# A decoder layer on one Trainium2 core: in the seven-product pairs, two of the four weight sums formed by an adding transfer instead of VectorE, more such pairs, and another order of pairs in the last matrix

## The chip, the core and the metric

The kernel runs on one core of a Trainium2 chip. The metric is device time in microseconds (us) of one execution, as the median over several executions. The engines have short names here: PE is TensorE, DVE is VectorE, ACT is ScalarE, POOL is GpSimd, and SP is SyncE, which issues nearly all of the DMA transfers. Every engine works through its own instructions strictly in program order, and an instruction whose semaphores have not come holds up all that stand behind it on that engine.

## The reference

One layer, 256 tokens, width 2048, all in float32. What matters here are its matrix products:

```python
h = rms_norm(x, mix_norm)
proj = h @ w_in                                  # attention, LRU and SSM inputs, and four gates of 2048 columns
gates = sigmoid(gate_logits)                     # (256, 4, 2048)
merged = sum(gates[b] * (branches[b] @ w_branch[b]) for b in range(4))
x = x + merged @ w_out
hf = rms_norm(x, ffn_norm)
gate, up = split(hf @ w_ffn_in)                  # 5632 columns each
return x + (silu(gate) * up) @ w_ffn_out         # 5632 -> 2048
```

## The kernel before

All weights are streamed once from HBM, and PE multiplies them with activations that stay in on-chip memory. Every product of two float32 numbers is made of three matmuls in a reduced format: a weight tile `wr` is split by ACT into a rounded part `wh` (line 209) and by DVE into the rest `wl` = `wr` - `wh` (line 214). The activations are split likewise, and PE adds up high·high, high·low and low·high (lines 202 to 204). One matmul takes 128 rows of the sum and 512 output columns for 128 tokens.

Gates, `w_ffn_in` and `w_ffn_out` go through `stream_pairs`. One step of it is a *pair* p: 256 rows of the inner dimension by 1024 columns, 1 MB, seen as a 2x2 block of weights `raw[:,0..3]` (128 rows by 512 columns each), against a 2x2 block of activations (two row blocks, two token blocks of 128). A *plain* pair makes the 2x2 block product with eight block products, that is 24 matmuls. A *seven* pair (p in `seven`) makes it with seven block products, 21 matmuls, as in Strassen's and Winograd's schemes. For that it needs sums of activation blocks, formed once, and four sums of weight blocks, formed for each pair: the tile `ws` (`t13`, one DVE instruction over 1024 columns, line 227), and two more of 512 columns each that overwrite `raw[:,0]` (line 233) and `raw[:,1]` (line 234). The four split steps of a seven pair are named a, b, c, d; `wl_fo_17c` is the split of `ws` of pair 17 in `w_ffn_out`, `wl_fo_17d` that of the two sums in `raw`. The first products of a seven pair use a and b; the fourth and fifth use c; the last two use d. Seven pairs collect four of their products in banks `m1`, `m5`, `m6`, `m7`, which are added into the results after the last seven pair of the column half (`shared_products`, and `mid` with lines 1125 to 1133 for `w_ffn_out`).

Stages: gates in eight stages (`ps_g`), each followed by a branch product (`ps_b`); then `w_out`; `w_ffn_in` in eleven steps j with eight pairs each (`fi`); `w_ffn_out` in two column halves, c = 0 and c = 1, of 22 pairs each (`fo`). `PLAN_GATE`, `SEVEN_IN`, `SEVEN_OUT` and `PLAN_OUT` are hand-written tables of the order of pairs and of which are seven pairs. A scheduler interleaves the instructions on each engine after them; weight work has high priority. Weight tiles come through three buffers (`wraw`), the split tiles through four of each kind. Activation sums for `w_ffn_out` are stored to HBM as they are formed (`sums`, line 1047) and read back two pairs at a time into `sr` (line 1111), then split into `sx_hi` and `sx_lo` (lines 1112, 1113). The residual is loaded whole into `x2o` (line 1100), and after each column half DVE adds the four result banks to it (line 1140), which also makes those banks free for the next half; line 1142 stores them.

Of the kernel before, what the change touches and what calls it, by code (L numbers as in the profile page):

```python
# [1240 lines left out]
```

## Time and profile before

| what | us |
|---|---|
| three runs: median (lowest to highest) | 1876.64 (1875.7 to 1876.91) |
| the profiled execution, its whole time | 1875.47 |
| span of the profiled execution | 1873.5 |
| PE busy | 1855.8, 99% of the span |
| DVE busy | 1414.0, 75% |
| ACT busy | 963.6, 51% |
| POOL busy | 175.3, 9% |
| mean DMA rate | 196 GB/s |

The profiled execution is 1.2 us below the median, and 2.0 us of its time lie outside the span. Matmuls are pipelined, so PE's busy time says that a matmul was in flight, not that PE was at its peak rate. A wait is listed with the instruction that ended last before the waiting one could start.

### The profile page before, as it was taken

How to read it: one execution, taken by the hardware profiler on the slowest of the kernel's cores; microseconds unless marked ns; L12 is line 12 of the kernel's file. 1: busy time of each engine (PE TensorE's matmuls, PEld its weight loads, DVE VectorE, ACT ScalarE, POOL GpSimd, SP SyncE). 2: the span in 40 equal slices, each digit the busy share in tenths (PEclk: the TensorE clock that was granted, in tenths of full speed). 3: DMA queues.
4: the chain of work that ended last, by engine and by line, in shares of the span. 5: the costliest groups of instructions: out<-in, count | busy, mean ns of one | idle time of the engine just before them, and what ended most of it. 6: DMA issues, size and time to landing. Idle time of an engine off the chain costs nothing.

```text
span 1873.5 us, 22243 instructions
## 1 busy us (share of the span) xinstructions
PE 1855.8 (99%) x8546; PEld 1546.1 (83%) x8546; DVE 1414.0 (75%) x1730; ACT 963.6 (51%) x1200; POOL 175.3 (9%) x152
## 2 busy tenths in 40 slices
...
GB/s 298 205 158 165 167 205 166 167 187 180 176 178 162 175 202 201 181 180 225 202 245 182 202 185 239 182 182 213 200 193 217 214 200 193 208 251 221 181 223 135
DMA packets 64567, 367.56 MB, mean 196 GB/s; under 512 B 7952, under 2 KB 17484, under 8 KB 23244
## 3 DMA queue, kind: packets, MB, share of 16 engines
...
## 4 chain that ended last, share of the span: by engine, by line
PE 96%; DVE 2%; DMA 1%; issue 0%; ACT 0%; SPq 0%; DVEq 0%
PE ps_fi L202 7%; PE ps_fi L203 7%; PE ps_fi L204 7%; PE ps_att L169 6%; PE ps_att L167 6%; PE ps_att L168 6%; PE ps_g L202 5%; PE ps_g L204 5%; PE ps_g L203 5%; PE ps_fo L202 3%; PE ps_fo L204 3%; PE ps_fo L203 3%; PE ps_b L203 2%; PE ps_b L204 2%; PE ps_b L202 2%; PE ps_ssm L167 2%
## 5 line engine op out<-in xcount | busy, mean ns | idle before, releaser
L161 DVE TENSOR_TENSOR wl_att<-wr_att,wh_att 128x1024 fp32r<-128x1024 f32 x128 | 159.6, 1250 | 92.5 <-ACT wh_att L159 92.3
L159 ACT ACTIVATE wh_att<-wr_att 128x1024 fp32r<-128x1024 f32 x128 | 135.4, 1060 | 163.9 <-PE ps_att L169 145.2
L167 PE MATMUL ps_att<-wh_att,hT_hi 128*128 128x512 f32 x512 | 206.6, 403 | 0.0
L169 PE MATMUL ps_att<-wh_att,hT_lo 128*128 128x512 f32 x512 | 200.2, 391 | 0.0
L168 PE MATMUL ps_att<-wl_att,hT_hi 128*128 128x512 f32 x512 | 199.8, 390 | 0.0
L169 PEld LDWEIGHTS ps_att<-wh_att,hT_lo 128*128 128x128 f32 x512 | 96.1, 188 | 20.7
L168 PEld LDWEIGHTS ps_att<-wl_att,hT_hi 128*128 128x128 f32 x512 | 96.4, 188 | 19.0
L167 PEld LDWEIGHTS ps_att<-wh_att,hT_hi 128*128 128x128 f32 x512 | 96.3, 188 | 18.8
L980 POOL TENSOR_TENSOR mg<-mg,gt 128x512 f32<-128x512 f32 x24 | 39.2, 1663 | 435.2 <-DVE gt L978 435.2
L167 PE MATMUL ps_ssm<-wh_ssm,hT_hi 128*128 128x384 f32 (+2 forms) x160 | 57.1, 357 | 7.3 <-ACT hT_hi L306 7.3
L161 DVE TENSOR_TENSOR wl_o<-wr_o,wh_o 128x1024 fp32r<-128x1024 f32 x32 | 40.8, 1281 | 26.2 <-ACT wh_o L159 26.1
L159 ACT ACTIVATE wh_o<-wr_o 128x1024 fp32r<-128x1024 f32 x32 | 33.8, 1060 | 48.3 <-PE ps_o L169 39.9
L784 POOL TENSOR_TENSOR sq_t<-tk_t 128x512 f32<-128x512 f32 (+3 forms) x32 | 32.5, 1025 | 272.2 <-ACT tk_t L779 272.0
L168 PE MATMUL ps_ssm<-wl_ssm,hT_hi 128*128 128x384 f32 (+2 forms) x160 | 56.5, 353 | 0.0
L169 PE MATMUL ps_ssm<-wh_ssm,hT_lo 128*128 128x384 f32 (+2 forms) x160 | 56.4, 353 | 0.0
L167 PE MATMUL ps_o<-wh_o,mT_hi 128*128 128x512 f32 x128 | 50.9, 397 | 0.0
L169 PE MATMUL ps_o<-wh_o,mT_lo 128*128 128x512 f32 x128 | 50.0, 391 | 0.0
L168 PE MATMUL ps_o<-wl_o,mT_hi 128*128 128x512 f32 x128 | 49.9, 390 | 0.0
L159 ACT ACTIVATE wh_ssm<-wr_ssm 128x768 fp32r<-128x768 f32 (+2 forms) x40 | 35.2, 889 | 26.0 <-PE ps_ssm L169 17.5
L161 DVE TENSOR_TENSOR wl_ssm<-wr_ssm,wh_ssm 128x768 fp32r<-128x768 f32 (+2 forms) x40 | 40.2, 1014 | 8.9 <-ACT wh_ssm L159 8.7
L159 ACT ACTIVATE wh_lru<-wr_lru 128x1024 fp32r<-128x1024 f32 x24 | 25.4, 1059 | 29.2 <-PE ps_lru L169 21.1
L167 PE MATMUL ps_lru<-wh_lru,hT_hi 128*128 128x512 f32 x96 | 39.3, 409 | 0.0
...
## 6 DMA issues: line engine op xcount, KB each, us to landing
wr_fi<-in_w_ffn_in SPq DMA_DIRECT2D x88, 1024.0 KB, 4.8
wr_att<-in_w_in SPq DMA_DIRECT2D x64, 1024.0 KB, 4.7
wr_g<-in_w_in SPq DMA_DIRECT2D x64, 1024.0 KB, 4.7
wr_fo<-in_w_ffn_out SPq DMA_DIRECT2D x44, 1024.0 KB, 5.0
wr_b<-in_w_branch SPq DMA_DIRECT2D x24, 1024.0 KB, 4.8
wr_o<-in_w_out SPq DMA_DIRECT2D x16, 1024.0 KB, 4.7
wr_lru<-in_w_in SPq DMA_DIRECT2D x12, 1024.0 KB, 4.7
...
```

The costliest lines, as they stand in the source:

```text
L159: A.activation(wh, rk, AF.Copy)
L161: V.tensor_tensor(wl, rk, wh.bitcast(F32), op=ALU.subtract)
L167: PE.matmul(o_ps, xh, wh[:, kk], start=(k == 0), stop=False)
L168: PE.matmul(o_ps, xh, wl[:, kk], start=False, stop=False)
L169: PE.matmul(o_ps, xl, wh[:, kk], start=False, stop=(k == kc - 1))
L202: PE.matmul(out, xh, wh[:, z], start=b not in begun, stop=False)
L203: PE.matmul(out, xh, wl[:, z], start=False, stop=False)
L204: PE.matmul(out, xl, wh[:, z], start=False, stop=left[b] == 0)
L784: G.tensor_tensor(sq[:, :m], tok[:, :m], tok[:, :m], op=ALU.mult)
L980: G.tensor_tensor(mg[:, n, t], mg[:, n, t], gt[n][t], op=ALU.add)
```

## The change

In a seven pair, `ws` is no longer formed by DVE. SP loads `raw[:,1:3]` of that pair a second time from HBM into `ws` (512 KB, line 230 after), and then POOL issues a transfer that reads `raw[:,0]` twice from HBM and adds it to what `ws` holds (512 KB, `accum_op=ALU.add`, line 233 after). `ws` gets two buffers. The signs follow: the sums are now plus where they were minus, and the activation sums and the collecting steps change sign to match. Of the four activation sums only three are kept beside the activations; the fourth takes the place of the block x(0,1) itself.

With the tables, 63 instead of 56 pairs are seven pairs: 21 instead of 20 in the gates, 22 instead of 20 in `w_ffn_in` (step j = 0 has them too), and ten instead of eight in each half of `w_ffn_out`. The order of pairs in `w_ffn_out` is another one. The sums for `w_ffn_in` stay on chip (no `sums_in`); `x2o` is loaded in two halves, the second after the stores of the first; `sr` is read in five transfers instead of four. Line numbers after: splits 212 and 217, sums 243 and 244 (233 and 234 before), adding results to the residual 1155 (1140 before).

```diff
-PLAN_GATE = {(0, 0): (range(8), ()), (0, 1): ((0, 2, 4, 5, 1, 6, 3, 7), (1, 3)), (1, 0): ((0, 2, 1, 4, 3, 6, 5, 7), SEVEN_GATE)}
+PLAN_GATE = {(0, 0): (range(8), ()), (0, 1): ((0, 2, 1, 4, 3, 6, 5, 7), SEVEN_GATE), (1, 0): ((0, 2, 1, 4, 3, 6, 5, 7), SEVEN_GATE)}
 SEVEN_IN = (3, 5)
-SEVEN_OUT = list(range(5, 20, 2))
-PLAN_OUT = (list(range(22)), [0, 1, 5, 2, 7, 3, 9, 4, 11, 6, 13, 8, 15, 10, 17, 12, 19, 14, 16, 18, 20, 21])
+SEVEN_OUT = list(range(1, 20, 2))
+PLAN_OUT = (
+    [0, 2, 4, 6, 1, 3, 8, 5, 10, 7, 9, 12, 11, 14, 13, 15, 16, 17, 19, 18, 20, 21],
+    [0, 1, 2, 3, 4, 5, 6, 7, 8, 9, 10, 11, 12, 13, 14, 15, 16, 17, 18, 19, 20, 21],
+)
...
                 if p in seven:
-                    t13 = pools["sum"].tile([P, 2, 512], F32, name=f"ws_{name}_{p}", tag="wsum")
-                    V.tensor_tensor(t13, raw[:, 1:3], raw[:, 0:1].to_broadcast([P, 2, 512]), op=ALU.subtract)
+                    t13 = pools["sum"].tile([P, 2, 512], F32, name=f"ws_{name}_{p}", tag="wsum", bufs=2)
+                    nc.sync.dma_start(
+                        t13, bass.AP(tensor=src.tensor, offset=src.offset + o + 512, ap=[[4 * 512, P], [512, 2], [1, 512]])
+                    )
+                    G.dma_start(
+                        t13,
+                        bass.AP(tensor=src.tensor, offset=src.offset + o, ap=[[4 * 512, P], [0, 2], [1, 512]]),
+                        accum_op=ALU.add,
+                    )
                     h11 = high(raw[:, 1:2], 1, 2, f"{name}_{p}a")
                     h2 = high(raw[:, 2:4], 0, 2, f"{name}_{p}b")
                     h13 = high(t13, 0, 2, f"{name}_{p}c")
                     w11 = low(*h11)
                     w2 = low(*h2)
                     V.tensor_tensor(raw[:, 0], t13[:, 1], raw[:, 1], op=ALU.add)
-                    V.tensor_tensor(raw[:, 1], raw[:, 3], raw[:, 0], op=ALU.subtract)
+                    V.tensor_tensor(raw[:, 1], raw[:, 3], raw[:, 0], op=ALU.add)
...
-                s = [(h[0][:, h[2], j], h[1][:, h[2], j]) for h in (seven[p],) for j in range(4)]
+                s = [(h[0][:, h[2], j], h[1][:, h[2], j]) for h in (seven[p],) for j in range(3)]
                 product("m1", x(0, 0), w11, 1)
                 product((0, 0), x(1, 0), w2, 1)
-                product((1, 0), s[3], w2, 0)
+                product((1, 0), x(0, 1), w2, 0)
...
-    def seven_operands(x, out, copy):
+    def seven_operands(x, out, p, hi, lo, copy=False):
 
 
         a11, a21, a12, a22 = x
         if copy:
             A.activation(out[:, 3], a21, AF.Copy)
             a21 = out[:, 3]
-        V.scalar_tensor_tensor(out[:, 0], a21, -1.0, a22, op0=ALU.mult, op1=ALU.subtract)
+        V.tensor_tensor(out[:, 0], a21, a22, op=ALU.subtract)
         V.tensor_tensor(out[:, 2], a11, a21, op=ALU.subtract)
-        V.scalar_tensor_tensor(out[:, 1], out[:, 0], -1.0, a11, op0=ALU.mult, op1=ALU.subtract)
-        V.tensor_tensor(out[:, 3], a12, out[:, 1], op=ALU.subtract)
+        V.tensor_tensor(out[:, 1], out[:, 0], a11, op=ALU.subtract)
+        V.tensor_tensor(out[:, 3], a12, out[:, 1], op=ALU.add)
+        A.activation(hi[:, 2 * p, P:S], out[:, 3], AF.Copy)
+        V.tensor_tensor(lo[:, 2 * p, P:S], out[:, 3], hi[:, 2 * p, P:S].bitcast(F32), op=ALU.subtract)
+
+    def split(hi, lo, x):
+        A.activation(hi, x, AF.Copy)
+        V.tensor_tensor(lo, x, hi.bitcast(F32), op=ALU.subtract)
 
...
-        V.tensor_tensor(g[1][0], m["m5"], g[1][0], op=ALU.add)
-        V.tensor_tensor(g[1][1], m["m5"], g[0][1], op=ALU.add)
+        V.tensor_tensor(g[1][0], m["m5"], g[1][0], op=ALU.subtract)
+        V.tensor_tensor(g[1][1], m["m5"], g[0][1], op=ALU.subtract)
...
-            hs2 = pools["sum"].tile([P, 2, 512], F32, name=f"hs{p}", tag="wsum")
+            hs2 = pools["sum"].tile([P, 2, 512], F32, name=f"hs{p}", tag="wsum", bufs=2)
             h, hs = hs2[:, 0].rearrange("p (k c) -> p k c", k=2), hs2[:, 1].rearrange("p (a b) -> p a b", b=P)
             V.tensor_tensor(h, actA_hi[:, s3].bitcast(F32), actA_lo[:, s3].bitcast(F32), op=ALU.add)
-            seven_operands([h[:, k, t * P : (t + 1) * P] for k in range(2) for t in range(T)], hs, False)
-            A.activation(hs_hi[:, i], hs, AF.Copy)
-            V.tensor_tensor(hs_lo[:, i], hs, hs_hi[:, i].bitcast(F32), op=ALU.subtract)
+            seven_operands([h[:, k, t * P : (t + 1) * P] for k in range(2) for t in range(T)], hs, p, actA_hi, actA_lo)
+            split(hs_hi[:, i], hs_lo[:, i], hs[:, 0:3])
...
+    def residual(c):
+        pools["x2"] = pools["out"].tile([P, T, 1024], F32, name=f"x2o{c}", tag="x2o")
+        nc.sync.dma_start(pools["x2"], x2_kept.rearrange("p (t d) -> p t d", t=T)[:, :, 1024 * c : 1024 * (c + 1)])
+        return
+        yield
+
...
     def sum_operands():
-        for i in range(0, len(SEVEN_OUT), 2):
-            sr = tmp(f"sr{i}").rearrange("p i (a b) -> p i a b", b=P)
+        for i in range(0, n, 2):
+            sr = tmp(f"sr{i}")[:, :, 0 : 3 * P].rearrange("p i (a b) -> p i a b", b=P)
             nc.sync.dma_start(sr, sums[i : i + 2].rearrange("i p (a b) -> p i a b", b=P))
-            A.activation(sx_hi[:, i : i + 2], sr, AF.Copy)
-            V.tensor_tensor(sx_lo[:, i : i + 2], sr, sx_hi[:, i : i + 2].bitcast(F32), op=ALU.subtract)
-            yield
```

The order of instructions is shown at three places. The first is DVE in the middle of the second half of `w_ffn_out`, in the split steps of pair 17. Before:

```order
L233 TENSOR_TENSOR wr_fo_17_14393<-ws_fo_17_14395,wr_fo_17_14393 128x512
L214 TENSOR_TENSOR wl_fo_17b<-wr_fo_17_14393,wh_fo_17b 128x1024
L234 TENSOR_TENSOR wr_fo_17_14393<-wr_fo_17_14393 128x512
L214 TENSOR_TENSOR wl_fo_17c<-ws_fo_17_14395,wh_fo_17c 128x1024
L227 TENSOR_TENSOR ws_fo_19_14472<-wr_fo_19_14470 128x1024
L214 TENSOR_TENSOR wl_fo_17d<-wr_fo_17_14393,wh_fo_17d 128x1024
L214 TENSOR_TENSOR wl_fo_12a<-wr_fo_12_14436,wh_fo_12a 128x1024
```

After:

```order
L217 TENSOR_TENSOR wl_fo_17a<-wr_fo_17_14679,wh_fo_17a 128x512
L244 TENSOR_TENSOR wr_fo_17_14679<-wr_fo_17_14679 128x512
L217 TENSOR_TENSOR wl_fo_17b<-wr_fo_17_14679,wh_fo_17b 128x1024
L217 TENSOR_TENSOR wl_fo_17c<-ws_fo_17_14681,wh_fo_17c 128x1024
L243 TENSOR_TENSOR wr_fo_19_14757<-ws_fo_19_14759,wr_fo_19_14757 128x512
L217 TENSOR_TENSOR wl_fo_17d<-wr_fo_17_14679,wh_fo_17d 128x1024
L217 TENSOR_TENSOR wl_fo_18a<-wr_fo_18_14723,wh_fo_18a 128x1024
```

Where DVE formed `ws` of pair 19 between steps c and d of pair 17, there now stands the sum of pair 19 that reads `ws`, and so waits for its adding transfer.

The second place is the border between the halves of `w_ffn_out`: DVE, from the split of the second half's first pair on; `x2o<-ps_fo_0` and `x2o<-ps_fo_1` are the additions that free the result banks of the first half. Before:

```order
L214 TENSOR_TENSOR wl_fo_0b<-wr_fo_0_13859,wh_fo_0b 128x1024
L1131 TENSOR_TENSOR x2o<-x2o,u_13771 128x512
L1132 TENSOR_TENSOR x2o<-x2o,u_13771 128x512
L227 TENSOR_TENSOR ws_fo_5_13929<-wr_fo_5_13927 128x1024
L1133 TENSOR_TENSOR x2o<-m_fo_13208,x2o 128x512
L233 TENSOR_TENSOR wr_fo_5_13927<-ws_fo_5_13929,wr_fo_5_13927 128x512
L1140 TENSOR_TENSOR x2o<-ps_fo_0_12977,x2o 128x512
L214 TENSOR_TENSOR wl_fo_1a<-wr_fo_1_13893,wh_fo_1a 128x1024
L214 TENSOR_TENSOR wl_fo_1b<-wr_fo_1_13893,wh_fo_1b 128x1024
L1140 TENSOR_TENSOR x2o<-ps_fo_0_12977,x2o 128x512
L1140 TENSOR_TENSOR x2o<-ps_fo_1_12978,x2o 128x512 x2
```

After:

```order
L217 TENSOR_TENSOR wl_fo_0a<-wr_fo_0_14015,wh_fo_0a 128x1024
L243 TENSOR_TENSOR wr_fo_1_14051<-ws_fo_1_14053,wr_fo_1_14051 128x512
L217 TENSOR_TENSOR wl_fo_0b<-wr_fo_0_14015,wh_fo_0b 128x1024
L1155 TENSOR_TENSOR x2o_13215<-ps_fo_0_13101,x2o_13215 128x512 x2
L217 TENSOR_TENSOR wl_fo_1a<-wr_fo_1_14051,wh_fo_1a 128x512
L1155 TENSOR_TENSOR x2o_13215<-ps_fo_1_13102,x2o_13215 128x512
L217 TENSOR_TENSOR wl_fo_1b<-wr_fo_1_14051,wh_fo_1b 128x1024
L244 TENSOR_TENSOR wr_fo_1_14051<-wr_fo_1_14051 128x512
L243 TENSOR_TENSOR wr_fo_3_14133<-ws_fo_3_14135,wr_fo_3_14133 128x512
L1155 TENSOR_TENSOR x2o_13215<-ps_fo_1_13102,x2o_13215 128x512
L217 TENSOR_TENSOR wl_fo_1c<-ws_fo_1_14053,wh_fo_1c 128x1024
```

One plain pair more lies between the last seven pair and this place, the additions out of the banks `m` are done before it, and ahead of the last of the four additions stand now a split, line 244, and line 243 of pair 3. On PE at this place, the second half's matmuls into its first result tile before the first one into `ps_fo_1` are these after the change (before, only six, all of pair 0's `wh_fo_0a` and `wl_fo_0a`):

```order
L206 MATMUL ps_fo_0_14013<-wl_fo_0b,gT_hi 128x512
L207 MATMUL ps_fo_0_14013<-wh_fo_0b,gT_lo 128x512
L205 MATMUL ps_fo_0_14013<-wh_fo_0b,gT_hi 128x512
L206 MATMUL ps_fo_0_14013<-wl_fo_0b,gT_hi 128x512
L207 MATMUL ps_fo_0_14013<-wh_fo_0b,gT_lo 128x512
L205 MATMUL m_fo_14074<-wh_fo_1a,gT_hi 128x512
L206 MATMUL m_fo_14074<-wl_fo_1a,gT_hi 128x512
L207 MATMUL m_fo_14074<-wh_fo_1a,gT_lo 128x512
L205 MATMUL ps_fo_0_14013<-wh_fo_1b,gT_hi 128x512
L206 MATMUL ps_fo_0_14013<-wl_fo_1b,gT_hi 128x512
L207 MATMUL ps_fo_0_14013<-wh_fo_1b,gT_lo 128x512
L205 MATMUL ps_fo_1_14014<-wh_fo_0a,gT_hi 128x512
```

Of these, with rows 1 to 12 of pair 0 (five of which are shown) and six of pair 1, there are 18, and the 19th waits for the last addition.

The third place is the beginning of `w_ffn_out` on DVE after the change; `sx_lo<-sr` are splits of activation sums read back from HBM:

```order
L217 TENSOR_TENSOR wl_fo_1a<-wr_fo_1_13279,wh_fo_1a 128x512
L244 TENSOR_TENSOR wr_fo_1_13279<-wr_fo_1_13279 128x512
L296 TENSOR_TENSOR sx_lo<-sr_13211,sx_hi 128x768
L217 TENSOR_TENSOR wl_fo_1b<-wr_fo_1_13279,wh_fo_1b 128x1024
L217 TENSOR_TENSOR wl_fo_1c<-ws_fo_1_13281,wh_fo_1c 128x1024
L296 TENSOR_TENSOR sx_lo<-sr_13217,sx_hi 128x768
L217 TENSOR_TENSOR wl_fo_1d<-wr_fo_1_13279,wh_fo_1d 128x1024
L217 TENSOR_TENSOR wl_fo_3a<-wr_fo_3_13327,wh_fo_3a 128x512
L217 TENSOR_TENSOR wl_fo_3b<-wr_fo_3_13327,wh_fo_3b 128x1024
L244 TENSOR_TENSOR wr_fo_3_13327<-wr_fo_3_13327 128x512
L217 TENSOR_TENSOR wl_fo_3c<-ws_fo_3_13329,wh_fo_3c 128x1024
L296 TENSOR_TENSOR sx_lo<-sr_13221,sx_hi 128x768
```

Before, the first seven pair was pair 5 in the sixth place of the order, with one such split in it; now it is pair 1 in the fifth place, followed at once by pair 3, and three of the splits stand within these two pairs.

## Rows read from the trace of the kernel before

**Rows 1.** Profile page: busy time of each engine, and the chain that ended last.

```profile
PE 1855.8 (99%) x8546; PEld 1546.1 (83%) x8546; DVE 1414.0 (75%) x1730; ACT 963.6 (51%) x1200; POOL 175.3 (9%) x152
...
PE 96%; DVE 2%; DMA 1%; issue 0%; ACT 0%; SPq 0%; DVEq 0%
```

**Rows 2.** Waits of PE: total us, times, longest us.

```profile
PE ps_ssm L167 <- ACT hT_hi L306: 7.3, 1, 7.3
PE ps_fo L202 <- DVE x2o L1140: 4.1, 1, 4.1
PE m_g L203 <- DVE wl_g_1d L214: 1.3, 2, 1.0
```

**Rows 3.** Timeline of PE at the border: start us, us, instruction, idle before.

```profile
1743.70 0.39 PE L203 MATMUL ps_fo<-wl_fo_21a,gT_hi 128*128 128x512 f32 x1
...
1747.33 0.39 PE L204 MATMUL ps_fo<-wh_fo_21b,gT_lo 128*128 128x512 f32 x1
1751.79 0.48 PE L202 MATMUL ps_fo<-wh_fo_0a,gT_hi 128*128 128x512 f32 x1 [4.07 <-DVE x2o L1140]
```

**Rows 4.** Windows there: us, busy us (instructions) of PE, PEld, DVE, ACT, POOL, granted clock, DMA.

```profile
1745.00:1750.00 5.00, 2.72 (x12) 1.91 (x11) 5.00 (x8) 2.00 (x2) 0.00 (x0) 1.00 0.64 238
1750.00:1755.00 5.00, 3.21 (x8) 2.58 (x9) 2.84 (x4) 0.00 (x0) 0.00 (x0) 0.71 0.61 167
1755.00:1760.00 5.00, 5.00 (x22) 4.09 (x21) 1.39 (x2) 1.50 (x2) 0.00 (x0) 0.95 0.71 225
```

**Rows 5.** Timeline of DVE at the border.

```profile
1733.26 1.23 DVE L214 TENSOR_TENSOR wl_fo_19d<-wr_fo,wh_fo_19d 128x1024 fp32r<-128x1024 f32 x1 [1.54 <-ACT wh_fo_19d L209]
...
1745.76 1.22 DVE L227 TENSOR_TENSOR ws_fo<-wr_fo 128x1024 f32<-128x1024 f32 x1
...
1750.96 1.88 DVE L1140 TENSOR_TENSOR x2o<-ps_fo,x2o 128x512 f32<-128x512 f32 x3
```

**Rows 6.** Timeline of ACT at the border.

```profile
1747.08 1.06 ACT L209 ACTIVATE wh_fo_1a<-wr_fo 128x1024 fp32r<-128x1024 f32 x1 [3.70 <-PE ps_fo L204]
1748.04 1.04 ACT L209 ACTIVATE wh_fo_1b<-wr_fo 128x1024 fp32r<-128x1024 f32 x1
```

**Rows 7.** Timeline of DVE within the second half.

```profile
1776.02 1.23 DVE L227 TENSOR_TENSOR ws_fo<-wr_fo 128x1024 f32<-128x1024 f32 x1 [1.65 <-DMA wr_fo<-in_w_ffn_out]
...
1814.76 1.23 DVE L214 TENSOR_TENSOR wl_fo_15c<-ws_fo,wh_fo_15c 128x1024 fp32r<-128x1024 f32 x1 [0.89 <-ACT wh_fo_15c L209]
...
1826.22 1.23 DVE L227 TENSOR_TENSOR ws_fo<-wr_fo 128x1024 f32<-128x1024 f32 x1
```

**Rows 8.** Timeline of PE within the second half.

```profile
1828.66 0.39 PE L203 MATMUL m_fo<-wl_fo_17c,sx_hi 128*128 128x512 f32 x1
...
1830.02 0.39 PE L203 MATMUL m_fo<-wl_fo_17d,sx_hi 128*128 128x512 f32 x1
```

**Rows 9.** DMA from 1765 to 1845 us: rate in 40 slices of 2 us, share of the queue, issues.

```profile
GB/s 0 70 369 389 225 4 0 217 406 369 57 0 123 410 418 102 0 225 422 385 25 0 176 426 406 41 0 156 406 438 49 8 135 406 406 102 0 66 393 377
...
q1 hardware_dynamic: 2236, 16.35, 53.9%
...
wr_fo<-in_w_ffn_out SPq DMA_DIRECT2D x17, 1024.0 KB, 5.0
```

**Rows 10.** Tile `sr` (512 KB loads): issue durations in ns, then us from issue to landing.

```profile
L1111 SPq DMA_DIRECT2D sr<-sums x4: 377/378/428, 1652.2 to 1680.2; - x4
...
DMA to landing us min/median/max: 3.6/5.7/7.8
```

**Rows 11.** Profile page: costliest groups, the POOL row (busy us, mean ns).

```profile
L980 POOL TENSOR_TENSOR mg<-mg,gt 128x512 f32<-128x512 f32 x24 | 39.2, 1663 | 435.2 <-DVE gt L978 435.2
```

**Rows 12.** Timelines of PE, DVE and ACT at the beginning of `w_ffn_out`.

```profile
1631.86 0.39 PE L202 MATMUL ps_fo<-wh_fo_0a,gT_hi 128*128 128x512 f32 x1
...
1645.76 0.68 DVE L1043 TENSOR_TENSOR gT_lo<-ftp,gT_hi 128x512 fp32r<-128x512 f32 x1
...
1660.00 1.06 ACT L1112 ACTIVATE sx_hi<-sr 128x1024 fp32r<-128x1024 f32 x1 [1.32 <-DMA sr<-sums]
```

More of the change, by code (lines that the diff above doesn't have):

```diff
@@ L1014, in hybrid @@
             mix.close()
+            xsp = pools["sum"] = ctx.enter_context(tc.tile_pool(name="xsp", bufs=1))
+            xs_hi, xs_lo = (xsp.tile([P, len(SEVEN_IN), 3, P], F32R, name=f"xs_{x}", tag=f"xs_{x}") for x in ("hi", "lo"))
             x2 = first_half.enter_context(tc.tile_pool(name="res", bufs=1)).tile([P, T, D], F32, name="x2", tag="x2")
@@ L1041, in gated_channels @@
             k0 = 4 * j + 2 * q
-            A.activation(gT_hi[:, k0 : k0 + 2], tp3, AF.Copy)
-            V.tensor_tensor(gT_lo[:, k0 : k0 + 2], tp3, gT_hi[:, k0 : k0 + 2].bitcast(F32), op=ALU.subtract)
+            split(gT_hi[:, k0 : k0 + 2], gT_lo[:, k0 : k0 + 2], tp.rearrange("p (b c) -> p b c", b=2))
             if k0 // 2 in SEVEN_OUT:
-                sraw = fin.tile([P, 4, P], F32, name=f"sraw{k0}", tag="sraw")
-                seven_operands([tp[:, i * P : (i + 1) * P] for i in range(4)], sraw, True)
-                nc.sync.dma_start(sums[SEVEN_OUT.index(k0 // 2)], sraw.rearrange("p a b -> p (a b)"))
@@ L1058, in normed_sums @@
+                nc.sync.dma_start(sums[SEVEN_OUT.index(k0 // 2)], sraw[:, 0:3].rearrange("p a b -> p (a b)"))
             yield
     for j in range(11):
-        gu, seven = [[None] * T, [None] * T], {}
-        if j:
-            sa, ua = (fin.tile([P, T, 512], F32, name=f"{x}{j}", tag=x) for x in ("sa", "ua"))
-            gu = [[sa[:, t] for t in range(T)], [ua[:, t] for t in range(T)]]
-            seven = {p: (xs_hi, xs_lo, i) for i, p in enumerate(SEVEN_IN)}
-        ps = stream_pairs(
-            a["w_ffn_in"], j * D * 1024, range(8), x2T_hi, x2T_lo, seven, f"fi{j}", lambda m, gu=gu: shared_products(m, gu)
-        )
@@ L1069, in hybrid @@
-        if j == 0:
-            drain("near")
-            mtp_stack.close()
-            first_half.close()
-            ffp = pools["sum"] = ctx.enter_context(tc.tile_pool(name="ffp", bufs=1))
-            gT_hi = ffp.tile([P, 44, S], F32R, name="gT_hi", tag="gT_hi")
-            gT_lo = ffp.tile([P, 44, S], F32R, name="gT_lo", tag="gT_lo")
-            fin = inner.enter_context(tc.tile_pool(name="fin", bufs=1, side="right"))
-            xs_hi, xs_lo = (fin.tile([P, len(SEVEN_IN), 4, P], F32R, name=f"xs_{x}", tag=f"xs_{x}") for x in ("hi", "lo"))
-            sa = fin.tile([P, T, 512], F32, name="sa0", tag="sa")
-            later(normed_sums(), "far")
@@ L1080, in hybrid, with take_out @@
-        th = ffp.tile([P, T, 512], F32, name=f"th{j}", tag="wsum")
+        gu = []
+        def take_out(m):
+            gu.extend(pools["in"].tile([P, T, 512], F32, name=f"{x}{j}", tag=x) for x in ("sa", "ua"))
+            shared_products(m, [[x[:, t] for t in range(T)] for x in gu])
+        seven = {p: (xs_hi, xs_lo, i) for i, p in enumerate(SEVEN_IN)}
+        ps = stream_pairs(a["w_ffn_in"], j * D * 1024, range(8), x2T_hi, x2T_lo, seven, f"fi{j}", take_out)
+        sa, ua = gu
+        th = xsp.tile([P, T, 512], F32, name=f"th{j}", tag="wsum", bufs=2)
@@ L1097, in second_half @@
         inner.close()
         pools["out"] = ctx.enter_context(tc.tile_pool(name="outp", bufs=1, side="right"))
-        pools["x2"] = pools["out"].tile([P, T, D], F32, name="x2o", tag="x2o")
-        nc.sync.dma_start(pools["x2"].rearrange("p t d -> p (t d)"), x2_kept)
-        later(sum_operands(), "far")
+        rest = sum_operands()
+        next(rest)
+        later(rest, "far")
+        return
[3 more added lines that the diff above has]
+        nc.sync.dma_start(pools["x2"], x2_kept.rearrange("p (t d) -> p t d", t=T)[:, :, 1024 * c : 1024 * (c + 1)])
@@ L1116, in columns @@
-    def columns(c):
-        return [[pools["x2"][:, t, 1024 * c + 512 * n : 1024 * c + 512 * (n + 1)] for t in range(T)] for n in range(2)]
-    later(second_half(), "near")
-    for c in range(2):
-        def mid(m):
-            xs = columns(c)
-            u = tmp(f"u{c}")
-            A.activation(u[:, 0], m["m1"], AF.Copy)
+            split(sx_hi[:, i : i + 2], sx_lo[:, i : i + 2], sr)
+            if i % 4 == 0:
+                yield
+    def columns():
+        return [[pools["x2"][:, t, 512 * n : 512 * (n + 1)] for t in range(T)] for n in range(2)]
```

75 lines of the change are left out of this document (43 added, 32 removed).

## Prediction

> **What bounds the kernel now.** I read the page first. PE is busy for 99% of the span and makes up 96% of the chain that ended last; DVE is busy for 75%, POOL for 9% [rows 1]. So time can come only from fewer matmuls, from PE's waits, or be lost to new ones. The waits of PE show how little there is to win: 12.7 us in four places [rows 2]. The first, 7.3 us at the start, is not touched. The second, 4.1 us, is the border between the halves of the last matrix, the third, 1.3 us, is in the gates. DVE's work as such bounds nothing: taking time off it is worth only what these two places hold.
>
> **Matmuls.** From 1743.70 to 1747.33 lie 16 steps, so one matmul costs PE 3.63/16 = 0.227 us [rows 3]. Seven more seven pairs save three matmuls each, 21 in all: **-4.8 us**. A plain pair is 24 x 0.227 = 5.4 us of PE, a seven pair 4.8, so one of each is 10.2.
>
> **The border.** PE idles 4.07 us there, until line 1140 has emptied the first result tile [rows 3]; then the granted clock is 0.71 and 0.95 as the mean of the next two windows [rows 4]: after the idle time it stood at the 1.2 GHz level for a while, then again at 2.4. From 1745 to 1760 it does 42 matmuls [rows 4]; at 0.227 us there would be 66. The place costs 24 x 0.227 = 5.4 us, not only the 4.07. The reason is DVE: from 1733.26 it works without a gap to the last addition at 1752.8 [rows 5], because the collecting steps of the last seven pair, a line 227 (1.22 us) and the weight splits come together. After the change one plain pair more lies between the last seven pair and the border, 5.4 us of cover in which DVE has two splits more (2.4 us), and line 227 is gone. So the first two additions should run as soon as PE finishes their banks, which are done halfway through the last pair.
>
> That doesn't close the place altogether, by the order shown in front. Let E be the end of the first half, 1747.56 before. ACT's split 1a starts 0.5 us ahead of E, since it needs a buffer that PE holds [rows 6]; as it is half as wide after the change, I let it end at E+0.1. Then DVE: split 1a and the third addition at 0.63 each (1.88/3 in [rows 5]), E+1.4; split 1b, after ACT's 1.04 [rows 6], 1.22, E+2.6; lines 244 and 243 and the fourth addition, E+4.5. PE has 18 matmuls that don't need that bank, 4.1 us. About 0.4 us is left, and line 243 of pair 3 waits there for a weight load and an adding transfer; I leave 1.0 us standing. Its bounds are nothing and the whole 4.0. Gain: 5.4 - 1.0 = **-4.4 us** (-5.4 to -1.4). The second residual load waits for the stores of the first half and holds up pair 4's weights on SP. PE comes to pair 4 after 5.4 + 4.8 + 5.4 + 4.8 = 20.4 us, and stores, load and splits need some 4.5 + 5.0 + 5.0 + 2.3 = 16.8 (5.0 for 1 MB, [rows 9]), so I cost that at nothing; without this cover it would be the difference.
>
> **The gates.** There PE waits 1.3 us for step d of pair 1 [rows 2], with line 227 of pair 3 ahead of it on DVE. It goes: **-1.3 us** (0 to -1.3).
>
> **The beginning of the last matrix.** The loads of activation sums share one buffer, each waits for the split of the one before, and three of five splits now stand within two seven pairs. The half begins at 1631.86 and the last split of the stage before ends at 1646.4 [rows 12]; that frees the space, so the first load can go out then, and PE reaches pair 1 after four plain pairs at 1653.7. With a landing of 3.6 to 5.7 us [rows 10] the first split is done at about 1652, the second load lands at 1655.6 to 1657.7, and with two instructions on ACT and two on DVE (about 1 us each) step d of pair 1 comes at about 1658.8 to 1660.9; PE wants it after 15 matmuls and two more steps, at 1657.6: 1.2 to 3.3 us. The third load repeats this in pair 3 with 4.8 us of PE's work between, 0 to 2.7 us more. Before, too, the first such split waited 1.32 us for its load [rows 12], but PE did not. I take **+3.0 us** (0 to 6).
>
> **The adding transfer.** No row shows one. What must be known is T, the time from the release of a buffer of `ws` (the end of step c, two seven pairs earlier) to the landing of the finished sum. Load: 512 KB land in 3.6 to 7.8 us [rows 10]; the queue has gaps, so 3.6. Issue by POOL: between SP's 0.38 for an issue [rows 10] and POOL's largest row, 1.66 [rows 11]; 1.0. Adding transfer: it writes 512 KB but must read what it adds to, so like 1 MB, 5.0 [rows 9], in bounds 3.6 to 7.8. T = 9.6 us (7.6 to 17.3). The two transfers run one behind the other, since the second must wait for the first.
>
> What T may be: step c of pair 15 ends at 1816.0 [rows 7], PE needs step d of pair 17 at 1830.0 [rows 8], and ahead of that go the split (1.2) and line 243 (0.6), so the sum of pair 19 must be there by 1828.2: 12.2 us. The gates have the same distance, with pairs 1, 3 and 5. In the first half line 243 stands ahead of step c three times: 1828.66 - 1.8 - 1816.0 = 10.9. `w_ffn_in` has two seven pairs in 43 us and more room. So T leaves 2.6 and 1.3 us, and I cost the wait at nothing; the cover is PE's work on a seven and a plain pair. Behind a late line 243 stand step d and all later splits, so PE would wait for all of the excess.
>
> **A rule that speaks against it.** The adding transfer counted twice, a period of 10.2 us in the second half carries 2.10 + 0.52 + 1.05 = 3.67 MB in place of 2.10, so the queue's share goes from 53.9% [rows 9] to about 94%. The Trainium skill has this as a rule in "Collectives: The Full Stack", section "The bandwidth ceiling: the fold count and why AG ≠ RS ≠ AR": an add inside a transfer costs two source reads, which halves the rate of the operation. No run here shows it yet. By the skill's "DMA: Bandwidth & Descriptors", section "Anatomy of one DMA — SWDGE (gpsimd) path", a transfer issued by POOL takes 2.0 us plus bytes at 436 GB/s; that is an estimate of 3.2 us for 512 KB, T would be 6.8, and the sum below would not move.
>
> That 94% is still 360 GB/s, and single slices reach 438 [rows 9]; the weight loads were late for line 227 by 1.65 us at one place already [rows 7], without PE waiting.
>
> **The sum.** -4.8 - 4.4 - 1.3 + 3.0 = -7.5 us. Against the profiled 1875.47 that gives 1868.0; the median lies 1.2 us higher, so **1869 us**. 0.2%, about what a measurement can tell from no change, is 3.75 us.
>
> **Rivals.**
>
> *The chain is just late.* If T exceeds 12.2 by x, eight gate stages lose x each, the second half x on every other seven pair (5x), the first half about 3(x + 1.3): 16x + 3.9. At T = 12.4 that eats the 7.5 us. For it: the share of 94% and weight loads of 1 MB beside the chain; against it: the gaps of some 4 us in each period [rows 9]. Below 12.2 only the 3(T - 10.9) of the first half counts. For T from 11.6 to 12.7 the time is 1871 to 1881, mostly no change.
>
> *The chain is far over, slower than before.* From T = 12.7 on the kernel is slower by 0.2%. At T = 14 the loss is 16 x 1.8 + 3.9 = 33 us, 25 net of the gain: 1902 us; at the upper bound, 17.3, some 85, 1954 us. It needs both transfers to be near the upper bounds of [rows 10], or an adding transfer twice as dear as a load of 1 MB. The Trainium skill's "DMA: Bandwidth & Descriptors", section "Issuing engines are not separate DMA queues", says that transfers issued by POOL run on the same 16 engines as SP's; by that rule the second queue brings no rate of its own, which would favour this rival.
>
> *The border stays.* If line 243 of pair 3 or its weight load is late by 3 us, PE idles again and the clock falls again as in [rows 4]: only 1.4 of 5.4 is won, 1872 us.
>
> **Chances.** Forecast 0.60, with a range of its own of 1865 to 1872.5: the border's and the beginning's bounds, of which not all fall the same way. Chain just late 0.13, far over 0.19, border stays 0.08. Faster by over 0.2% (below 1872.9): 0.58 of the forecast, 0.05 of the border, 0.03 of just late, 0.66. Slower (above 1880.4): 0.19, and 0.01 of just late's end, 0.20. No change: 0.14. The range goes from 1864 to 1884. Where the beginning costs nothing and the border closes, the time is 1865, and I give 1 us for the scatter of runs; 1884 is T = 12.9, and beyond it lies most of "far over".
>
> **What would show it.** Right: PE has 21 matmuls fewer, its idle time at the border is 1 us or less with the clock at 1.00, no wait for step d of pair 1 in the gates, DMA share near 0.9 in the second half, and line 243 waits little. Wrong: PE or DVE waits for line 243 or step d with the adding transfer as the releaser, in gates and last matrix alike; POOL's transfers landing more than 7.6 us after their issue; or waits of 3 us and more at the first two seven pairs of the last matrix.

## The result and the profile after

The changed kernel takes 2013.99 us (median of 4 runs, 2011.57 to 2016.8) against 1876.53: a ratio of 1.0734, with a 95% interval of 1.0715 to 1.0752. It is 137 us slower; I had forecast 1869. The profiled execution has a span of 2015.0 us, 141.5 more than before.

The page of the changed kernel, its busy times and the chain that ended last:

```profile
PE 1901.9 (94%) x8525; PEld 1562.4 (78%) x8525; DVE 1375.2 (68%) x1734; ACT 972.8 (48%) x1233; POOL 251.2 (12%) x215
...
PE 65%; DMA 20%; DVE 9%; issue 4%; ACT 1%; DVEq 0%; POOL 0%; POOLq 0%; ACTq 0%; SPq 0%
```

PE has 21 matmuls fewer than in [rows 1], as forecast. But the chain, 96% PE before, is now 20% DMA and 9% DVE. The waits of PE say where (us in total, times, longest):

```profile
PE m_g L206 <- DVE wl_g_3d L217: 28.1, 7, 6.7
PE m_fi L206 <- DVE wl_fi_3c L217: 19.2, 10, 2.1
...
PE m_fo L206 <- DVE wl_fo_13c L217: 5.8, 1, 5.8
...
PE ps_fo L205 <- DVE x2o L1155: 2.3, 1, 2.3
```

Those of [rows 2] were 12.7 us; these and the smaller ones add up to 107.2. Most of them are for steps c and d of seven pairs, in all three stages that have them. DVE's waits between 1760 and 2012 us name what DVE waits for in line 243:

```profile
DVE wr_fo L243 <- DMA ws_fo<-in_w_ffn_out: 55.0, 12, 8.4
DVE wr_fo L243 <- DMA wr_fo<-in_w_ffn_out: 9.0, 3, 3.8
```

And the price of the adding transfer: the tile `ws_fo`, POOL's issues (ns) and the time to landing (us), then the load ahead of it by SP, then three rows of the DMA list: the 1 MB weight loads, and the two transfers in the gates.

```profile
L233 POOL DMA_DIRECT2D ws_fo<-in_w_ffn_out x20: 1203/1203/1222, 1721.1 to 1972.5; - x20
...
DMA to landing us min/median/max: 7.5/11.5/13.4
```

```profile
DMA to landing us min/median/max: 3.7/5.7/8.1
```

```profile
wr_fo<-in_w_ffn_out SPq DMA_DIRECT2D x44, 1024.0 KB, 7.6
...
ws_g<-in_w_in SPq DMA_DIRECT2D x21, 512.0 KB, 4.6
...
ws_g<-in_w_in POOLq DMA_DIRECT2D x21, 512.0 KB, 10.8
```

The time to landing counts from the start of the issue, so POOL's 1.2 us lie within the 11.5. By these medians T, in the last matrix, is 5.7 + 11.5 = 17.2 us where I had taken 3.6 + 1.0 + 5.0 = 9.6 against an allowance of 12.2; in the gates it is 4.6 + 10.8 = 15.4. One such chain, on DVE, SP, POOL and DVE again:

```profile
1895.15 1.22 DVE L217 TENSOR_TENSOR wl_fo_5c<-ws_fo,wh_fo_5c 128x1024 fp32r<-128x1024 f32 x1
...
1896.39 0.33 SPq L230 DMA_DIRECT2D ws_fo<-in_w_ffn_out  x1
...
1902.52 1.20 POOL L233 DMA_DIRECT2D ws_fo<-in_w_ffn_out  x1 [8.08 <-DMA ws_fo<-in_w_ffn_out]
...
1914.08 0.69 DVE L243 TENSOR_TENSOR wr_fo<-ws_fo,wr_fo 128x512 f32<-128x512 f32 x1 [2.19 <-DMA ws_fo<-in_w_ffn_out]
```

Step c of pair 5 frees the buffer at 1896.37, SP's load leaves at once, and the finished sum for pair 9 is there 17.7 us later.

One wait of PE, and the windows around it:

```profile
1898.57 0.39 PE L205 MATMUL m_fo<-wh_fo_5d,sx_hi 128*128 128x512 f32 x1
1902.62 0.79 PE L206 MATMUL m_fo<-wl_fo_5d,sx_hi 128*128 128x512 f32 x1 [3.67 <-DVE wl_fo_5d L217]
1903.22 0.63 PE L207 MATMUL m_fo<-wh_fo_5d,sx_lo 128*128 128x512 f32 x1
...
1908.34 0.51 PE L207 MATMUL ps_fo<-wh_fo_6a,gT_lo 128*128 128x512 f32 x1
1908.69 0.40 PE L205 MATMUL ps_fo<-wh_fo_6a,gT_hi 128*128 128x512 f32 x1
```

```profile
1890.00:1900.00 10.00, 8.95 (x39) 7.02 (x38) 5.11 (x6) 6.21 (x7) 1.20 (x1) 1.00 0.97 304
1900.00:1910.00 10.00, 7.38 (x20) 5.88 (x21) 6.61 (x7) 1.48 (x2) 1.20 (x1) 0.66 0.67 173
```

PE stands for 3.67 us, then does the next matmuls at 0.43 us each, the 1.2 GHz level, until 1908.3: 20 matmuls in a window that holds 44. From 1898.57 to 1908.69 it does 15 steps, 3.4 us at 0.227 each, in 10.1 us, so this wait cost 3.0 us beyond its own length. The gates with their branches, `w_ffn_in` and `w_ffn_out` of the changed kernel, and the first and last of them in e2 (told below), which has the same matmuls:

```profile
586.50:1107.70 521.20, 489.46 (x2119) 401.63 (x2118) 350.69 (x390) 248.20 (x283) 65.58 (x51) 0.97 0.70 227
...
1199.50:1716.80 517.30, 491.54 (x2135) 393.48 (x2135) 380.71 (x471) 251.19 (x299) 24.91 (x21) 0.99 0.69 228
1716.80:2015.00 298.20, 250.05 (x1005) 198.22 (x1003) 185.82 (x202) 126.25 (x135) 24.08 (x20) 0.92 0.76 234
```

```profile
587.40:1062.40 475.00, 474.22 (x2119) 391.89 (x2118) 375.10 (x411) 248.71 (x283) 37.42 (x28) 1.00 0.54 198
...
1629.60:1869.90 240.30, 231.22 (x1005) 188.03 (x1003) 206.38 (x222) 126.84 (x135) 0.00 (x0) 0.99 0.55 203
```

For the same matmuls PE is busy 15.2 us longer in the gates and 18.8 longer in the last matrix, at granted clocks of 0.97 and 0.92 in place of 1.00 and 0.99. Over the whole span its busy time grew from 1855.8 to 1901.9 us. So waits that grew by 94.5 us, with a busy time that grew by 46.1, make up nearly all of the 141.5 us of span. In `w_ffn_in`, where no wait is longer than 2.1 us, the clock is 0.99; PE is busy 16.2 us longer there than in e2 (475.3), of which 1% of clock over 517 us makes some 5. The rest was not taken apart.

By stages, from the first matmul of one to the first of the next (us; the experiments are told below):

| kernel | gates and branches | `w_out` | `w_ffn_in` | `w_ffn_out` | PE's waits |
|---|---|---|---|---|---|
| before | 476.8 | 91.9 | 477.0 | 241.6 | 12.7 |
| changed | 521.2 | 91.8 | 517.3 | 298.2 | 107.2 |
| sums by DVE (e2) | 475.0 | 91.9 | 475.3 | 240.3 | 12.6 |
| POOL's transfer plain (e3) | 493.8 | 91.8 | 498.7 | 276.5 | 61.6 |
| third buffer in the last matrix (e4) | 514.6 | 91.9 | 521.0 | 275.3 | 88.6 |
| load only (e5) | 474.5 | 91.9 | 475.5 | 239.6 | 12.5 |
| tanh apart (e6) | 518.1 | 91.8 | 489.8 | 286.9 | 86.8 |
| DVE, sums read pair by pair (e7) | 475.1 | 91.8 | 475.5 | 234.2 | 9.2 |
| less weight load in the last matrix (e8) | 511.3 | 91.8 | 521.5 | 292.9 | 100.9 |

`w_out`, which has no seven pairs, doesn't move; the three others lose 44.4, 40.3 and 56.6 us.

### The profile page after: what moved, and what is told of

It reads as the page before. It is cut to its first block, busy times and chain, and to the rows that moved or that the text cites. A ratio compares the mean times of both kernels' runs of the same rounds, so it can differ in the third digit from the quotient of the medians.

```text
span 2015.0 us, 22519 instructions
## 1 busy us (share of the span) xinstructions
PE 1901.9 (94%) x8525; PEld 1562.4 (78%) x8525; DVE 1375.2 (68%) x1734; ACT 972.8 (48%) x1233; POOL 251.2 (12%) x215
## 3 DMA queue, kind: packets, MB, share of 16 engines
q0 software_dynamic: 17136, 33.03, 10.2%
## 4 chain that ended last, share of the span: by engine, by line
PE 65%; DMA 20%; DVE 9%; issue 4%; ACT 1%; DVEq 0%; POOL 0%; POOLq 0%; ACTq 0%; SPq 0%
PE ps_att L172 6%; PE ps_att L170 6%; PE ps_att L171 6%; DMA ws_fo<-in_w_ffn_out 5%; DMA ws_fi<-in_w_ffn_in 5%; DMA ws_g<-in_w_in 4%; PE ps_g L206 4%; PE ps_g L205 3%; PE ps_g L207 3%; PE ps_fi L207 3%; PE ps_fi L206 3%; PE ps_fi L205 3%; DMA wr_fo<-in_w_ffn_out 3%; DMA wr_fi<-in_w_ffn_in 2%; PE ps_b L205 2%
## 5 line engine op out<-in xcount | busy, mean ns | idle before, releaser
L170 PEld LDWEIGHTS ps_att<-wh_att,hT_hi 128*128 128x128 f32 x512 | 96.3, 188 | 18.8
L233 POOL DMA_DIRECT2D ws_fi<-in_w_ffn_in x22 | 26.6, 1228 | 448.4 <-DVE ua L1092 447.4
L233 POOL DMA_DIRECT2D ws_g<-in_w_in x21 | 25.4, 1209 | 288.4 <-DMA ws_g<-in_w_in 96.1
L243 DVE TENSOR_TENSOR wr_fo<-ws_fo,wr_fo 128x512 f32<-128x512 f32 x20 | 13.8, 691 | 69.1 <-DMA ws_fo<-in_w_ffn_out 58.8
L243 DVE TENSOR_TENSOR wr_fi<-ws_fi,wr_fi 128x512 f32<-128x512 f32 x22 | 15.2, 691 | 63.8 <-DMA ws_fi<-in_w_ffn_in 50.7
L233 POOL DMA_DIRECT2D ws_fo<-in_w_ffn_out x20 | 24.1, 1204 | 273.3 <-DMA ws_fo<-in_w_ffn_out 92.8
L243 DVE TENSOR_TENSOR wr_g<-ws_g,wr_g 128x512 f32<-128x512 f32 x21 | 14.5, 689 | 59.8 <-DMA ws_g<-in_w_in 45.6
```

Of the source, the lines that this page charges most:

```text
L170: PE.matmul(o_ps, xh, wh[:, kk], start=(k == 0), stop=False)
L233: G.dma_start(t13, bass.AP(tensor=src.tensor, offset=src.offset + o, ap=[[4 * 512, P], [0, 2], [1, 512]]), accum_op=ALU.add,)
L243: V.tensor_tensor(raw[:, 0], t13[:, 1], raw[:, 1], op=ALU.add)
```

## The experiments

**e1: the price by itself.** A kernel of chains of transfers, in which each waits for the one before:

```diff
+    for _ in range(N):
+        G.dma_start(t, ap(rep), accum_op=ALU.add)
...
+    for i in range(22):
+        nc.sync.dma_start(w[i % 3], ap([[512, 4], [1, 512]]))
+        if i % 3 == 0 and i < 18:
+            G.dma_start(t, ap(rep), accum_op=ALU.add)
```

> This kernel leaves out the whole layer: it only makes chains of transfers, in which each waits for the landing of the one before, and stores the input. 512 KB each: plain loads issued by SP, plain loads issued by POOL, adding transfers that read one row block twice, adding transfers that read two row blocks, adding transfers of 256 KB; then plain and adding transfers issued by POOL beside a stream of 1 MB loads of SP. Theory A (the addition is slow by itself): plain loads land in 3.5 to 5 us from either engine, adding transfers alone in 6.5 us or more, and beside the stream in 10 or more. Theory B (only the crowding is to blame): adding transfers alone land within 1 us of plain ones of POOL, 4 to 5 us, and in about 10 beside the stream; the plain ones of POOL then take about as long beside the stream. Theory C (POOL's path is slow, whatever is transferred): plain loads issued by POOL take 6.5 us or more alone. If 256 KB of adding take half of what 512 KB take, the time goes with the bytes; if they take nearly the same, it is a fixed delay.

POOL's timeline: two issues each of plain transfers alone, adding ones alone, plain ones of 512 KB beside SP's loads, and adding ones beside them:

```profile
50.04 0.53 POOL L58 DMA_DIRECT2D pool_plain<-in_w_ffn_out  x1 [3.54 <-DMA pool_plain<-in_w_ffn_out]
54.09 0.53 POOL L58 DMA_DIRECT2D pool_plain<-in_w_ffn_out  x1 [3.52 <-DMA pool_plain<-in_w_ffn_out]
...
83.55 1.18 POOL L61 DMA_DIRECT2D pool_add_rep<-in_w_ffn_out  x1 [4.85 <-DMA pool_add_rep<-in_w_ffn_out]
89.55 1.18 POOL L61 DMA_DIRECT2D pool_add_rep<-in_w_ffn_out  x1 [4.81 <-DMA pool_add_rep<-in_w_ffn_out]
...
196.41 0.53 POOL L74 DMA_DIRECT2D beside_plain<-in_w_ffn_out  x1 [8.04 <-DMA beside_plain<-in_w_ffn_out]
204.75 0.53 POOL L74 DMA_DIRECT2D beside_plain<-in_w_ffn_out  x1 [7.81 <-DMA beside_plain<-in_w_ffn_out]
...
258.40 1.17 POOL L80 DMA_DIRECT2D beside_add<-in_w_ffn_out  x1 [11.27 <-DMA beside_add<-in_w_ffn_out]
270.84 1.17 POOL L80 DMA_DIRECT2D beside_add<-in_w_ffn_out  x1 [11.27 <-DMA beside_add<-in_w_ffn_out]
```

From one issue to the next an adding transfer takes 89.55 - 83.55 = 6.0 us alone, just the 1.0 + 5.0 of the prediction, and 270.84 - 258.40 = 12.4 beside a full stream of weight loads. Theory A falls: alone it isn't slow. Theory C falls too: a plain transfer of POOL takes 4.05 us. Theory B holds in part. Both kinds are long only beside the stream, but there a plain one takes 8.3 to 9.0 us and an adding one 12.4, so the addition has a share of its own. Alone, too, POOL waits 4.81 us behind the issue of an adding one and 3.52 behind a plain one, more than the 1 us apart that I had allowed. In the two other chains an adding transfer that reads two row blocks takes 5.7 us, and one of 256 KB takes 4.2: its time is neither fixed nor in proportion to the bytes.

**e2: sums by DVE, all else as changed.**

```diff
-                    nc.sync.dma_start(t13, ...)
-                    G.dma_start(t13, ..., accum_op=ALU.add)
+                    V.tensor_tensor(t13, raw[:, 1:3], raw[:, 0:1].to_broadcast([P, 2, 512]), op=ALU.add)
```

> The changed kernel with its tables, orders and buffers, but the sums of two weight blocks formed by DVE again, in one instruction of 1.22 us per seven pair, in place of the second load and the adding transfer. If the adding transfers cause the whole loss, the terms of the prediction that don't hang on them stand: 21 matmuls less (-4.8), some of the border (-1 to -4), the beginning of the last matrix (0 to +6), so 1868 to 1876 us, and PE's waits are below 20 us. Rival: the new order of pairs, the two buffers or the shared sums cost time themselves; then it is above 1880 us, and PE waits where it waits in the changed kernel, in the first seven pairs of the last matrix above all.

1870.63 us (11 runs), ratio to the kernel before 0.997, interval 0.9961 to 0.9979: 0.3% faster, and the interval leaves out 1. PE's waits, the largest:

```profile
PE ps_ssm L170 <- ACT hT_hi L315: 6.9, 1, 6.9
PE m_fo L205 <- ACT wh_fo_1d L212: 1.1, 1, 1.1
...
PE ps_fo L205 <- DVE x2o L1148: 0.8, 1, 0.8
PE m_fo L206 <- DVE wl_fo_1d L217: 0.8, 1, 0.8
PE m_g L206 <- DVE wl_g_3d L217: 0.6, 1, 0.6
PE m_fo L205 <- ACT wh_fo_1c L212: 0.5, 1, 0.5
```

The rival falls. Tables, order and shared sums are no part of the loss; all of it comes with the way the weight sums are formed.

**e3: POOL's transfer without the addition** (the sums are then not the sums).

```diff
-                        accum_op=ALU.add,
```

> The changed kernel, but POOL's transfer doesn't add: it overwrites, with the same bytes from the same place and the same waits ahead of it, so the weight sums are left out and the output is another one. Theory A or B by the addition: POOL's transfer lands in 4 to 6 us instead of 9.6 to 11.5, T is 10 to 12, and the kernel takes 1865 to 1895 us. Theory C (POOL's path) or pure crowding by the added 66 MB: it lands in 9 us or more as before, and the kernel stays above 1980 us.

1950.13 us (one run), in neither of my two ranges. In `w_ffn_out` the transfer lands in 7.9 us (median) instead of 11.5, and POOL's issue takes 0.72 instead of 1.20. T is 5.5 + 7.9 = 13.4, still above 12.2. My lower range, 1865 to 1895, took a landing of 4 to 6 us for granted, which e1 shows only for a transfer alone. Leaving out the addition gives back 64 of the 137 us; 74 are lost even with the plain transfer in its place.

**e5: the load only**, without POOL's transfer.

```diff
-                    G.dma_start(t13, ..., accum_op=ALU.add)
```

> The changed kernel with the second load by SP but without POOL's transfer behind it, so one of the addends of the weight sums is left out. The bytes of the second load stay (33 MB), the chain has one link less. If PE waits because two transfers and an issue stand in a row, T is now the load alone, 4 to 6 us, well under 12.2: 1866 to 1876 us, PE's waits below 20 us. If it waits because more bytes share the DMA engines, a half of the bytes leaves about a half of what the plain transfer of POOL lost (74 us): 1900 us or more.

1870.18 us (one run), with PE's waits at 12.5 us: the kernel is as fast as with DVE's sums. 33 MB more on SP's queue cost nothing; the loss comes with POOL's transfer behind the load. This run takes out that link and its 33 MB together, so it doesn't say which of the two counts; e4 bears on that. The load lands in 3.6 us here; with POOL's transfers about it was 5.7.

**e4: a third buffer for the weight sums, in the last matrix.** The line that gives the activation sums of `w_ffn_in` the same tag, `xs`, is left out here:

```diff
+                    third = name[:2] == "fo" and sevens.index(i) % 3 == 2
-                    t13 = pools["sum"].tile([P, 2, 512], F32, name=f"ws_{name}_{p}", tag="wsum", bufs=2)
+                    t13 = pools["sum"].tile([P, 2, 512], F32, name=f"ws_{name}_{p}", tag="xs" if third else "wsum", ...)
```

> The changed kernel with a third buffer for the weight sums, in the last matrix alone (it takes the space of the activation sums of the matrix before). A buffer then comes free three seven pairs ahead instead of two, which gives the chain of load, issue and adding transfer about 22 us there in place of 12. If the length of that chain is what PE waits for, the last matrix goes from 298 us to 240 to 255, and the kernel to 1957 to 1972 us. If the DMA engines have too much to move, the chain only begins earlier and each transfer takes longer: the last matrix stays above 275 us, the kernel above 1990.

1991.69 us (one run); the last matrix takes 275.3 us, 23 less. That is just inside the second of my two cases (above 275 and 1990), though the adding transfer takes no longer than before: it lands in 11.3 us. DVE's waits from 1760 to 1985 us:

```profile
DVE wr_fo L247 <- DMA wr_fo<-in_w_ffn_out: 32.9, 10, 5.9
DVE wr_fo L247 <- DMA ws_fo<-in_w_ffn_out: 3.8, 1, 3.8
```

Line 247 is line 243 of the changed kernel. With a longer allowance the wait for the adding transfer is nearly gone, 55.0 to 3.8 us, and the same instruction now waits for the weight load, 9.0 to 32.9. Those loads are in a row of their own, of three buffers, and land in 7.2 us (5.0 in [rows 9]). So the length of the chain was the first wait. That the second one, right behind it, is crowding is my reading of the 7.2 against 5.0; no run tried it by itself.

**e6: tanh's values apart from the weight sums, in `w_ffn_in`.**

```diff
-        th = xsp.tile([P, T, 512], F32, name=f"th{j}", tag="wsum", bufs=2)
+            th = pools["in"].tile([P, 512], F32, name=f"th{j}{t}", tag="th", bufs=1)
```

> The changed kernel, but in w_ffn_in the values of tanh have a buffer of their own of half the size (one token block at a time) and no longer take one of the two buffers of the weight sums. POOL can then issue its transfers for pairs 3 and 5 when step c of the column block before is done, some 25 us earlier. If the late start is what costs w_ffn_in its 42 us against the kernel with DVE's sums (517 against 475), it falls to 475 to 485 us and the kernel to 1972 to 1984 us. If crowding of the DMA engines costs it, wherever the transfers begin, it stays above 505 us and the kernel above 2000.

1975.78 us (one run), as expected; `w_ffn_in` takes 489.8 us, above the 475 to 485 of my first case. In the changed kernel POOL's timeline between 1300 and 1345 us has one row:

```profile
1341.35 2.46 POOL L233 DMA_DIRECT2D ws_fi<-in_w_ffn_in  x2 [44.44 <-DVE ua L1092]
```

Both adding transfers of a column block leave together and late. The load ahead of the second one leaves at 1337.53, right behind line 1091, the last reader of `th` (1337.50): `th` held its buffer. The load ahead of the first one, which stands at the head of what PE's wait for step 3c goes back to, had its buffer free since step c of pair 5 (1321.39); it stands behind weight loads in SP's order and leaves at 1334.72. With `th` apart SP's order is another one, and the loads leave at 1306.68 and 1316.71, right behind steps 3c and 5c of the block before. The adding transfers follow as the loads land, 11 us apart (the releasers named are splits that ended at about the same time):

```profile
1310.85 1.20 POOL L233 DMA_DIRECT2D ws_fi<-in_w_ffn_in  x1 [34.64 <-DVE wl_fi_4a L217]
1322.25 1.20 POOL L233 DMA_DIRECT2D ws_fi<-in_w_ffn_in  x1 [10.20 <-DVE wl_fi_6b L217]
```

`w_ffn_in` falls from 517.3 to 489.8 us. Of the 14.5 that are left over e2's 475.3, 10.4 are a new wait of PE for line 1092, which came with this edit:

```profile
PE ps_fi L205 <- DVE ua L1092: 10.4, 10, 2.5
```

**e8: half the weight load in the plain pairs of the last matrix** (half of their product is left out).

```diff
+                z = 2 if name[:2] == "fo" and p not in seven else 4
```

> The changed kernel, but in the last matrix the plain pairs load only the first half of their weights and use it twice, so a half of their product is left out; the work of all engines and the chain of the sums stay. Each period of a seven and a plain pair moves 0.5 MB less on SP's queue. If the adding transfers are long because they share the DMA engines with weight loads, they land in 8 to 10 us in the last matrix instead of 11.5, and it takes 255 to 275 us instead of 298. If they are long by themselves there, or the wait is not theirs, it stays above 290 us.

2006.69 us (one run); the last matrix takes 292.9 us, 5.3 less, in the second of my cases (above 290). The landing falls as expected, to 9.9 us, but the load ahead lands in 6.3, so T is 16.2 instead of 17.2. I had looked at one link and forgotten the other. By itself 5.3 us says little: in e6, where the last matrix is not changed, it takes 286.9, 11.3 less, and why is open. But there T is 4.9 + 10.9 = 15.8, so over e3, e6, e8 and the changed kernel the last matrix takes the longer the longer T is: 276.5, 286.9, 292.9 and 298.2 us at 13.4, 15.8, 16.2 and 17.2.

**e7: activation sums read back pair by pair**, on top of e2, into two buffers of half the size. Not shown here: a line by which these reads and splits may also come in between the seven pairs of the first half.

```diff
-        for i in range(0, n, 2):
-            sr = tmp(f"sr{i}")[:, :, 0 : 3 * P].rearrange("p i (a b) -> p i a b", b=P)
+        for i in range(n):
+            sr = tmp(f"sr{i}")[:, 0 : 3 * P].rearrange("p (a b) -> p a b", b=P)
```

> The kernel with DVE's weight sums again, with one step more: the activation sums for the last matrix are read back for each pair by itself into one of two buffers, instead of for two pairs at a time into a single one. PE waited some 2.4 us there in the first seven pair, for loads that wait for the split before them. If that series of loads and splits is the cause, 1 to 2.4 us go, 1868 to 1870 us. If not (ten loads and ten splits cost more than five), it is the same or slower, 1870 to 1874 us.

1865.43 us (5 runs), ratio to the kernel before 0.9943, interval 0.9929 to 0.9957: 10.9 us faster, the best version here. PE's waits are four rows:

```profile
PE ps_ssm L170 <- ACT hT_hi L315: 7.4, 1, 7.4
PE m_g L206 <- DVE wl_g_3d L217: 1.1, 1, 1.1
PE m_fo L205 <- ACT wh_fo_1c L212: 0.5, 1, 0.5
PE m_fo L206 <- DVE wl_fo_5d L217: 0.2, 1, 0.2
```

The gain over e2 is 5.2 us, twice what I had counted. The waits in the last matrix fell by 3.1 us, and that stage by 6.1. A good part of the rest is time at the lower clock after those waits. The same five us near its beginning, in e2 and then in e7:

```profile
1658.00:1663.00 5.00, 4.61 (x13) 3.65 (x14) 5.00 (x7) 4.20 (x5) 0.00 (x0) 0.66 0.87 283
```

```profile
1658.00:1663.00 5.00, 4.87 (x21) 3.61 (x20) 5.00 (x6) 4.20 (x7) 0.00 (x0) 1.00 0.68 246
```

## Why the prediction was wrong

**The step that failed** is the price of T, "T = 9.6 us (7.6 to 17.3)". It was priced from transfers that ran with little beside them. The adding transfer itself, "like 1 MB, 5.0", is right alone: 6.0 us with its issue in e1, as taken. In the kernel it lands in 11.5, its issue included. "The queue has gaps, so 3.6" failed for the load ahead of it (5.7): as I read it, the gaps are there because the transfers wait for buffers that come free at about the same time, and the new ones begin then too; this was argued, not tried. At 17.2 us T is at my upper bound, 17.3, for which the rival had 1954 us. e1 shows the dependence on what runs beside; e5 shows that without POOL's transfer the time is back.

The Trainium skill's "DMA: Bandwidth & Descriptors", section "Issuing engines are not separate DMA queues", which I had put with the rival, agrees with e1: beside SP's stream a plain transfer of POOL needs 8.3 to 9.0 us in place of 4.05. The Trainium skill's "Collectives: The Full Stack", section "The bandwidth ceiling: the fold count and why AG ≠ RS ≠ AR", has an add halve the rate, for a ReduceScatter over a ring of cores. Here the queue of the adding transfers holds the engines for 10.2% of 2015.0 us for 33.03 MB, 161 GB/s, and in e3 the same bytes without the addition for 6.5% of 1948.4, 261 GB/s: 0.6, near that rule. But the same bytes also come in 17136 packets with the addition and 9072 without, and no run separates the two. These are the rows, of the changed kernel and of e3:

```profile
q0 software_dynamic: 17136, 33.03, 10.2%
```

```profile
q0 software_dynamic: 9072, 33.03, 6.5%
```

**A second step failed in `w_ffn_in`:** "has two seven pairs in 43 us and more room". The room was not there: the stage lost 42 us (517.3 - 475.3). One of the two buffers is also `th`'s, until the end of the block before, and the load for pair 3 stood behind weight loads in SP's order. With `th` apart both loads leave earlier and e6 gives back 27.5 us; of the rest 10.4 are a wait that e6 itself brought, and 4.1 stay open. The buffer's other user stood in the kernel.

**The mechanism of the rival held; the rule for its cost lacked a part of the price.** "Behind a late line 243 stand step d and all later splits, so PE would wait for all of the excess" is what the waits show. 16x + 3.9 counts eight gate stages, but only seven have seven pairs, 21 in all, so it should be 15x + 3.9. At the measured T that gives 7 x 3.2 + 8 x 5.0 + 3.9 = 66 us for gates and last matrix, and PE's waits there grew from e2's 4.4 to 74.9, by 70.5. In e3 the same sum, with T at 13.0 and 13.4, gives only 19 where the waits grew by 37, so medians are a rough measure of it. Against e2 the two stages lost 46.2 + 57.9 = 104 us. What the rule lacks is the 34 us by which the matmuls got slower, at the lower clock after the waits, which I had counted at the border and not here. The rival "far over" had the right sign and place, though its largest time, 1954, is 60 us short; I gave it 0.19.

**The other terms held in their sum**, as e2 and e5 show, at 1870.6 and 1870.2 us, inside the forecast's own range; in e2 the gates and `w_ffn_in` gained 3.5 us where their terms gave 3.3, but the last matrix 1.3 where its terms gave 4.1. Matmuls: 21 fewer. The border: "I leave 1.0 us standing", 0.8 in e2. The beginning, "+3.0 us": 1.1 + 0.8 + 0.5 = 2.4 us of waits in pair 1, and e7 confirms its cause, loads that wait for splits. But it too left out the clock: with e7's edit the last matrix got 6.1 us shorter, so the term was nearer to its upper bound of 6. The gates: pair 1's wait went, and one of 0.6 came for pair 3.
